# Delta-rule sequences: the layout of a PSUM bank and the time at which outputs leave it

## The chip, the cores and the metric

The kernel runs on one core of a Trainium2 chip. The metric is the device time of one execution in microseconds (us). A core has a matrix engine (TensorE, PE in the profile, its weight loads PEld), a vector engine (DVE), a scalar engine (ACT), GpSimd (POOL) and a queue engine (SP) that issues DMAs. Each engine works through its own instructions in order and waits for others by semaphores. [...]

## The reference

A decoder trunk of four layers over 1024 tokens of width 1024. The token mixers are a gated convolution (layers 0 and 3), a diagonal state-space layer (1) and RWKV-7 time mixing (2). Each layer ends with a gated addition and a LayerNorm. The change is in layer 2, whose core is a recurrence over tokens with a 64x64 state per head, 16 heads:

```python
def _rwkv_step(state, inp):
    r_t, w_t, k_t, v_t, kk_t, a_t = inp
    sa = jnp.einsum("bhvk,bhk->bhv", state, -kk_t)
    state = (state * w_t[:, :, None, :] + sa[..., None] * (kk_t * a_t)[:, :, None, :]
             + v_t[..., None] * k_t[:, :, None, :])
    out = jnp.einsum("bhvk,bhk->bhv", state, r_t)
    return state, out
```

The outputs are then normalised over the 64 values of each head and token (`mu_o`, `var_o`), scaled, joined with a bonus term and gated.

## The kernel before

Layer 2 treats the tokens in two halves of 512 (`h`) and the heads in eight pairs (`m`), so there are 16 sequences. A sequence is eight chunks of 64 tokens (`c`), with the two heads of the pair side by side. The recurrence in a chunk is written as matrices, in four generators per pair:

- `prep` makes the products within a chunk (`scr`, the L1982 matmuls), transposes `kb` to `kbt` (L2006) and prepares `uv` (L2017).
- `tsolve` solves a triangular system on DVE.
- `join` (L2057) assembles that inverse as `tt` with the matmuls `zp` (L2076) and `tp` (L2084). It then opens two PSUM banks `p1`, each with a small matmul by `zero` (L2094). The product of `tt` and `uv` is put into them (L2100), and the matmuls `a2` (L2106) give the part that ACT copies into `ra` (L2109).
- `seq` (L2114) runs the chunks one after the other. For each, `p1` gets `ra` times the state (L2127), ACT copies one half of its rows back as the chunk's `uv` (L2128), `p2` is `kbt` times `uv` (L2131), and two DVE instructions put `p2` into the state `st` (L2134). The next chunk's `p1` needs that state, so this is a chain PE, ACT, PE, DVE.

The parity `w = c % 2` decides which 64 partitions hold a chunk's `uv` and which its output. One bank holds the four even chunks, the other the four odd ones, so both are open from `join` to the end of `seq`. After the last chunk, 16 matmuls with `scr` (L2141) complete the outputs of all eight, and ACT copies them to `o` (L2144).

Behind that come eight squares with sums (`gsq`, L2155), an addition on POOL (`gn_q`, L2156), an inverse root on ACT and DVE, a multiplication of `o` on POOL (L2162), transposes on PE (`otp`, L2169), a scaling on ACT (`yt`), two POOL operations and a DMA out. `o`, `gsq` and `yt` share the tag `t_u` with two buffers.

While the sequence of pair `m-1` runs, the program works on pair `m`: projections (`sp`, 128x512 matmuls of L326 to L328, three for each product), `prep` and `tsolve`. The tile scheduler sets the order on each engine from priorities: `prio(..., PJ)` for `prep` and `join` and `prio(..., PS)` for `seq`, with 600 and 300. After the last pair of the first half come the projections of the second half (`pwa`, L1640), after that of the second half the output projection `op` and the gate `gp`, with POOL adds `rp` (L920).

Of the kernel before, what the change touches and what calls it, by code (L numbers as in the profile page):

```python
# [8 lines left out]
F32 = mybir.dt.float32  # L9
# [6 lines left out]
P = 128  # L16
NB = 8
T = 1024
HT = 512
# [1902 lines left out]
def inner_setup(S, rg, T_):  # L1922
    nc = S.nc
    V, G, SC = nc.vector, nc.gpsimd, nc.scalar
# [21 lines left out]
    rows_b = (slice(0, 64), slice(64, P))  # L1946
    rows_k = (slice(64, P), slice(0, 64))
# [3 lines left out]
    def aux(nm):  # L1951
        return S.paux.tile([P, HT], F32, tag="aux", name=nm)

    def sq(nm):
        return S.pseq.tile([P, HT], F32, tag="sq", name=nm)

    zero = rg.tile([P, 2], F32, tag="zero", name="zero")
# [99 lines left out]
    def join(m, h, R):  # L2057
        ra, ti = R.ra, R.ti
        tt = slot(S, ("a0", "a1")[h], "tt")
        tt = R.tt = tt.rearrange("p (h c) -> p h c", h=8)  # L2060
# [13 lines left out]
        for e in range(8):  # L2074
            for w in range(2):
                nc.tensor.matmul(ps[w][q1[w], e * 32:(e + 1) * 32], R.m10[q0[w], e, :], t1[q0[w], e, :],  # L2076
                                 start=True, stop=True)
# [4 lines left out]
        for e in range(8):  # L2082
            for w in range(2):
                nc.tensor.matmul(ps[w][q0[w], e * 32:(e + 1) * 32], zs[q1[w], e, :], tt[q1[w], e, 32:64],  # L2084
                                 start=True, stop=True)
# [3 lines left out]

        an = R.ant.rearrange("p (c s) -> p c s", c=4)  # L2090
        r5 = ra.rearrange("p (c w) s -> p c w s", w=2)
        R.p1 = [S.pseq.tile([P, 4, P], F32, tag="p1", name="p1", bufs=2) for w in range(2)]
        for w in range(2):
            nc.tensor.matmul(R.p1[w][:, 0, 0:2], S.ident, zero, start=True, stop=False, skip_group_check=True)  # L2094
        ps = [aux("a2"), aux("a2")]
        for c2 in range(4):
            for hd in range(2):
                for w in range(2):
                    rb, cs = rows_b[w], slice(hd * 64, hd * 64 + 64)
                    nc.tensor.matmul(R.p1[w][rb, c2, cs], tt[rb, 2 * c2 + hd, :], R.uv[w][rb, c2, cs],  # L2100
                                     start=False, stop=False, skip_group_check=True)
        for c2 in range(4):
            for hd in range(2):
                for w in range(2):
                    rb = rows_b[w]
# [8 lines left out]
    def seq(m, h, R, dVT, dST, dBV, dZ, dY):  # L2114
# [2 lines left out]
            G.memset(st, 0.0)  # L2117
        else:
            nc.sync.dma_start(st, dST[m][:])
        ot = S.tmp.tile([P, HT], F32, tag="t_u", name="o")  # L2120
        o4 = ot.rearrange("p (c s) -> p c s", c=4)
        for c in range(8):
            w, c2 = c % 2, c // 2
            rb = rows_b[w]
            uv = R.uv[w][:, c2, :]
            p1 = R.p1[w][:, c2, :]
            nc.tensor.matmul(p1, R.ra[:, c, :], st, start=False, stop=False, skip_group_check=True)  # L2127
            SC.copy(uv[rb, :], p1[rb, :])  # L2128
            yield
            p2 = sq("p2")  # L2130
            last = nc.tensor.matmul(p2[:, 0:P], R.kbt[c // 4][:, c % 4, :], uv, start=True, stop=True)  # L2131
            for hd in range(2):
                cs = slice(hd * 64, hd * 64 + 64)
                V.scalar_tensor_tensor(st[cs, cs], st[cs, cs], R.pc[cs, c:c + 1], p2[cs, cs], ALU.mult, ALU.add)  # L2134
            yield
        with S.tc.issue_after(last.ins):
            for c2 in range(4):
                for hd in range(2):
                    for w in range(2):
                        cs = slice(hd * 64, hd * 64 + 64)  # L2140
                        nc.tensor.matmul(R.p1[w][rows_k[w], c2, cs], R.scr[w][:, c2, hd, :], R.uv[w][:, c2, cs],  # L2141
                                         start=False, stop=True, skip_group_check=True)
        for w in range(2):
            SC.copy(o4[rows_k[w]], R.p1[w][rows_k[w]])  # L2144
        if h == 0:
            nc.sync.dma_start(dST[m][:], st)

# [1 line left out]
        o = ot.rearrange("p (g v) -> p g v", v=64)  # L2149
# [56 lines left out]
```

## Time and profile before

| what | value |
|---|---|
| median of three runs | 2838.6 us (2838.0 to 2841.43) |
| the profiled execution | 2839.38 us, span 2837.7 us |
| mean granted TensorE clock | 0.963 |
| first and last p1 of the sequences | 1348.1 and 2106.0 us from the span's start |
| output copies L2144 | 32, of 580 ns |
| squares L2155 | 128, of 241 ns |

A row of waits gives an instruction, whom it waited for, the total in us, the number of waits and the longest. A timeline row gives start, duration, engine, line, operation, what it writes and reads, and in brackets the idle time of its engine ahead of it. Buffer numbers are left out, so `p` stands for p1 at L2127 and for p2 at L2131. A matmul of fp32 data leaves two records.

### The profile page before, as it was taken

The page shows a single profiled execution, that of the slowest core. Times are in us where ns is not written, and L with a number is a line of the kernel's source. Part 1 is how long each engine was busy: PE and PEld are TensorE (multiplying, and loading weights), DVE is VectorE, ACT ScalarE, POOL GpSimd, SP SyncE. Part 2 cuts the span into 40 slices and gives each one's busy share as a digit, 9 for nine tenths or more (in the row PEclk, how much of TensorE's full clock was granted, in tenths as well). Part 3 has the DMA queues.
Part 4 walks back from the last instruction along what each step waited for, and adds up shares of the span by engine and source line. Part 5 has one row for each costly group of instructions (what it writes and reads, how often), then busy time and mean ns, then how long its engine had stood idle before and what let it go on. Part 6 is the DMA issues. An engine that isn't in the chain of part 4 may idle for free.

```text
span 2837.7 us, 40655 instructions
## 1 busy us (share of the span) xinstructions
PE 2681.3 (94%) x14939; PEld 2127.4 (75%) x14939; DVE 1994.8 (70%) x3584; ACT 1163.1 (41%) x2211; POOL 646.9 (23%) x696
## 2 busy tenths in 40 slices
PE   8999999999999999899888799898889999999998
PEld 6877788778877888576667567666768777887887
DVE  6787865477657346888888667888756678876544
ACT  3333322242135223656555476555534343224332
POOL 1143422221116132203333110333232211111000
PEclk9999999999999999999997799999699999999999
DMA  5333322347884333473222245223234433324511
GB/s 168 98 97 97 95 75 66 89 142 212 220 240 140 104 94 122 117 233 107 78 85 87 63 151 170 84 91 89 78 100 135 144 111 111 108 71 129 171 64 38
DMA packets 463128, 331.56 MB, mean 117 GB/s; under 512 B 49449, under 2 KB 398929, under 8 KB 462929
## 3 DMA queue, kind: packets, MB, share of 16 engines
q1 hardware_dynamic: 462928, 328.96, 38.3%
q8 instruction: 118, 1.93, 0.3%
q14 instruction: 82, 0.66, 0.1%
HBM read 250.77 MB, written 77.59 MB: 116 GB/s over the span
## 4 chain that ended last, share of the span: by engine, by line
PE 70%; DVE 16%; ACT 4%; issue 4%; DMA 3%; POOL 3%; SPq 0%; DVEq 0%; POOLq 0%; ACTq 0%
PE op L327 3%; PE op L326 3%; PE op L328 3%; PE gp L328 3%; PE gp L327 3%; PE gp L326 3%; PE sp L326 3%; PE sp L327 3%; PE sp L328 2%; DVE tv L2048 2%; PE qa L508 2%; PE qa L506 2%; PE qa L507 2%; PE zp L326 2%; PE zp L328 2%
## 5 line engine op out<-in xcount | busy, mean ns | idle before, releaser
L299 DVE TENSOR_TENSOR wl<-wraw,wh 128x1024 fp32r<-128x1024 f32 x255 | 331.1, 1299 | 217.9 <-ACT wh L298 214.2
L298 ACT CAST wh<-wraw 128x1024 fp32r<-128x1024 f32 x255 | 267.5, 1049 | 517.7 <-PE gp L327 191.5
L905 POOL TENSOR_TENSOR ln_s<-ln_s,rp 128x512 f32<-128x512 f32 x42 | 60.0, 1429 | 209.8 <-DVE rp L901 209.8
L2134 DVE SCALAR_TENSOR_TENSOR state<-state,pc,p 64x64 f32<-64x64 f32 x256 | 71.1, 278 | 46.9 <-PE p L2131 42.1
L2048 DVE TENSOR_TENSOR tv<-ti,mi 128x128 f32<-128x128 f32 (+3 forms) x128 | 97.8, 764 | 2.4
L2127 PE MATMUL p<-state,ra 128*128 128x128 f32 x256 | 65.6, 343 | 28.8 <-DVE state L2134 26.7
L2128 ACT COPY uv<-p 64x128 f32<-64x128 f32 x128 | 33.1, 259 | 136.5 <-PE p L2127 135.8
L2127 PEld LDWEIGHTS p<-state,ra 128*128 128x128 f32 x256 | 45.8, 217 | 54.1 <-DVE state L2134 44.0
L1982 PEld LDWEIGHTS s<-ra,kb 64*128 64x128 f32 x512 | 64.7, 213 | 20.4 <-ACT scr L1988 6.2
L1982 PE MATMUL s<-ra,kb 64*128 64x128 f32 x512 | 75.2, 314 | 4.1 <-DVE kb L1738 1.9
L328 PE MATMUL gp<-r_0h,wl 128*128 128x512 f32 x192 | 77.5, 404 | 0.0
L327 PE MATMUL gp<-r_0l,wh 128*128 128x512 f32 x192 | 76.8, 400 | 0.0
L326 PE MATMUL gp<-r_0h,wh 128*128 128x512 f32 x192 | 76.6, 399 | 0.0
L326 PE MATMUL gp<-r_1h,wh 128*128 128x512 f32 x192 | 76.4, 398 | 0.0
L920 POOL TENSOR_TENSOR rp<-r_0h,r_0l 128x512 f32<-128x512 f32 x24 | 36.3, 1544 | 174.9 <-PE op L327 174.9
L328 PE MATMUL gp<-r_1h,wl 128*128 128x512 f32 x192 | 76.1, 396 | 0.1
L2131 PE MATMUL p<-uv,kbt 128*128 128x128 f32 x256 | 66.8, 347 | 9.9 <-ACT uv L2128 9.8
L327 PE MATMUL gp<-r_1l,wh 128*128 128x512 f32 x192 | 75.6, 394 | 0.0
L2131 PEld LDWEIGHTS p<-uv,kbt 128*128 128x128 f32 x256 | 44.5, 212 | 37.7 <-ACT uv L2128 31.9
L1991 POOL TENSOR_TENSOR scr<-scr,mask 128x512 f32<-128x512 f32 x32 | 46.0, 1436 | 55.4 <-ACT scr L1988 55.2
L326 PE MATMUL sp<-xs0h,wh 128*128 128x512 f32 x128 | 56.1, 438 | 2.6 <-DVE aq L1720 2.2
L327 PE MATMUL sp<-xs0l,wh 128*128 128x512 f32 x128 | 56.0, 437 | 1.9 <-DVE xs0l L195 1.9
(851 smaller groups left out, 8669.6 us busy)
## 6 DMA issues: line engine op xcount, KB each, us to landing
wraw<-in_conv_w_in_dram SPq DMA_DIRECT2D x84, 512.0 KB
wraw<-in_rwkv_w_rkvz_dram SPq DMA_DIRECT2D x64, 512.0 KB
wraw<-in_ple_gate_dram SPq DMA_DIRECT2D x56, 512.0 KB
wraw<-in_conv_w_out_dram SPq DMA_DIRECT2D x24, 512.0 KB
xt<-xd SPq DMA_DIRECT2D x48, 256.0 KB
wraw<-in_ssm_w_in_dram SPq DMA_DIRECT2D x21, 512.0 KB
xd<-rp SPq DMA_DIRECT2D x40, 256.0 KB
wraw<-in_rwkv_w_out_dram SPq DMA_DIRECT2D x16, 512.0 KB
```

Source lines behind the costliest of these rows:

```text
L298: nc.scalar.copy(wh, raw)
L299: nc.vector.tensor_tensor(wl, raw, f32(wh[:]), ALU.subtract)
L326: nc.tensor.matmul(ps, lh, xh, start=(n == 0), stop=False)
L327: nc.tensor.matmul(ps, lh, xl, start=False, stop=False)
L328: nc.tensor.matmul(ps, ll, xh, start=False, stop=(n == kt - 1))
L506: nc.tensor.matmul(ps, wh[:, k0 + k, :], xh, start=first and k == 0, stop=False, skip_group_check=True)
L905: nc.gpsimd.tensor_tensor(s, s, rs, ALU.add)
L1982: nc.tensor.matmul(pss[hd][:, c * P:(c + 1) * P], kb[rows, 2 * c + w, :], ra[rows, 2 * c + w, :], start=True, stop=True)
L2048: V.tensor_tensor(tv, ti[:, b:8, 4 * b:4 * b + 4].unsqueeze(2).to_broadcast([P, n, c, 4]), mi[:, 4 * b:4 * b + 4, 0:c].rearrange("p q c -> ...
L2127: nc.tensor.matmul(p1, R.ra[:, c, :], st, start=False, stop=False, skip_group_check=True)
L2131: last = nc.tensor.matmul(p2[:, 0:P], R.kbt[c // 4][:, c % 4, :], uv, start=True, stop=True)
L2134: V.scalar_tensor_tensor(st[cs, cs], st[cs, cs], R.pc[cs, c:c + 1], p2[cs, cs], ALU.mult, ALU.add)
```

## The change

A PSUM bank `p1` now holds chunks 0 to 3 of both parities, and a second one chunks 4 to 7. A function `bank` in `seq` opens one and puts the products of `tt` and `uv` into it; the first is opened at the start of `seq`, the second within it, behind chunk 2's copy. `join` no longer touches p1. After chunk 3 and after chunk 7, eight matmuls complete the outputs of four chunks, and ACT copies them to `o` in two pieces of 64x256. `o` gets a tag of its own with two buffers, and the scratch for dynamic DMAs in SBUF is set to 1024 bytes per partition, where the default stood.

```diff
--- before.py
+++ after.py
@@ -2089,16 +2089,7 @@
 
         an = R.ant.rearrange("p (c s) -> p c s", c=4)
         r5 = ra.rearrange("p (c w) s -> p c w s", w=2)
-        R.p1 = [S.pseq.tile([P, 4, P], F32, tag="p1", name="p1", bufs=2) for w in range(2)]
-        for w in range(2):
-            nc.tensor.matmul(R.p1[w][:, 0, 0:2], S.ident, zero, start=True, stop=False, skip_group_check=True)
         ps = [aux("a2"), aux("a2")]
-        for c2 in range(4):
-            for hd in range(2):
-                for w in range(2):
-                    rb, cs = rows_b[w], slice(hd * 64, hd * 64 + 64)
-                    nc.tensor.matmul(R.p1[w][rb, c2, cs], tt[rb, 2 * c2 + hd, :], R.uv[w][rb, c2, cs],
-                                     start=False, stop=False, skip_group_check=True)
         for c2 in range(4):
             for hd in range(2):
                 for w in range(2):
@@ -2117,31 +2108,47 @@
             G.memset(st, 0.0)
         else:
             nc.sync.dma_start(st, dST[m][:])
-        ot = S.tmp.tile([P, HT], F32, tag="t_u", name="o")
+        ot = rg.tile([P, HT], F32, tag="o", name="o", bufs=2)
         o4 = ot.rearrange("p (c s) -> p c s", c=4)
+
+        def bank(ph):
+
+            p1 = S.pseq.tile([P, 2, 2, P], F32, tag="p1", name="p1", bufs=2)
+            nc.tensor.matmul(p1[:, 0, 0, 0:2], S.ident, zero, start=True, stop=False, skip_group_check=True)
+            for c2 in range(2):
+                for hd in range(2):
+                    for w in range(2):
+                        rb, cs = rows_b[w], slice(hd * 64, hd * 64 + 64)
+                        nc.tensor.matmul(p1[rb, w, c2, cs], R.tt[rb, 2 * (2 * ph + c2) + hd, :],
+                                         R.uv[w][rb, 2 * ph + c2, cs], start=False, stop=False, skip_group_check=True)
+            return p1
+        p1s = [bank(0)]
         for c in range(8):
-            w, c2 = c % 2, c // 2
+            w, c2, ph = c % 2, c // 2, c // 4
             rb = rows_b[w]
             uv = R.uv[w][:, c2, :]
-            p1 = R.p1[w][:, c2, :]
+            p1 = p1s[ph][:, w, c2 % 2, :]
             nc.tensor.matmul(p1, R.ra[:, c, :], st, start=False, stop=False, skip_group_check=True)
             SC.copy(uv[rb, :], p1[rb, :])
             yield
+            if c == 2:
+                p1s.append(bank(1))
             p2 = sq("p2")
             last = nc.tensor.matmul(p2[:, 0:P], R.kbt[c // 4][:, c % 4, :], uv, start=True, stop=True)
             for hd in range(2):
                 cs = slice(hd * 64, hd * 64 + 64)
                 V.scalar_tensor_tensor(st[cs, cs], st[cs, cs], R.pc[cs, c:c + 1], p2[cs, cs], ALU.mult, ALU.add)
+            if c % 4 == 3:
+                with S.tc.issue_after(last.ins):
+                    for k in range(2):
+                        for hd in range(2):
+                            for w in range(2):
+                                cs = slice(hd * 64, hd * 64 + 64)
+                                nc.tensor.matmul(p1s[ph][rows_k[w], w, k, cs], R.scr[w][:, 2 * ph + k, hd, :],
+                                                 R.uv[w][:, 2 * ph + k, cs], start=False, stop=True, skip_group_check=True)
+                for w in range(2):
+                    SC.copy(o4[rows_k[w], 2 * ph:2 * ph + 2, :], p1s[ph][rows_k[w], w])
             yield
-        with S.tc.issue_after(last.ins):
-            for c2 in range(4):
-                for hd in range(2):
-                    for w in range(2):
-                        cs = slice(hd * 64, hd * 64 + 64)
-                        nc.tensor.matmul(R.p1[w][rows_k[w], c2, cs], R.scr[w][:, c2, hd, :], R.uv[w][:, c2, cs],
-                                         start=False, stop=True, skip_group_check=True)
-        for w in range(2):
-            SC.copy(o4[rows_k[w]], R.p1[w][rows_k[w]])
         if h == 0:
             nc.sync.dma_start(dST[m][:], st)
 
@@ -2192,7 +2199,7 @@
     import concourse.bacc as _bacc
     from concourse.bass_utils import run_bass_kernel_spmd as _run
 
-    nc = _bacc.Bacc("TRN2", target_bir_lowering=False, num_devices=1)
+    nc = _bacc.Bacc("TRN2", target_bir_lowering=False, num_devices=1, dynamic_dma_scratch_size=1024)
     arrays, aps = {}, {}
     for name in _INS:
         a = _np.ascontiguousarray(inputs[name])
```

The scheduler orders the engines anew, from the first sequence to the end of layer 2. Three places show how. The numbers behind `p_` tell buffers apart.

PE in pair 4 of the second half, from the p1 matmul of chunk 0 to that of chunk 1. Before:

```order
L2127 MATMUL p_18065<-state,ra 128x128
L1716 MATMUL pss<-c_ones,sq 128x2 x4
L2169 MATMUL otp<-ident,o 128x128 x4
L2131 MATMUL p_18165<-uv,kbt 128x128
L1734 MATMUL prn<-ident,rnb 128x128 x4
L1745 MATMUL antp<-ident,aq 128x128
L2127 MATMUL p_18066<-state,ra 128x128
```

In the change (p1 is L2131, p2 is L2137, the bank's first products L2122):

```order
L2131 MATMUL p_18167<-state,ra 128x128
L2122 MATMUL p_18210<-uv,tt 64x64 x2
L1716 MATMUL pss<-c_ones,sq 128x2 x4
L328 MATMUL sp<-xs0h,wl 128x512
L326 MATMUL sp<-xs0h,wh 128x512
L2137 MATMUL p_18179<-uv,kbt 128x128
L327 MATMUL sp<-xs0l,wh 128x512
L328 MATMUL sp<-xs0h,wl 128x512
L326 MATMUL sp<-xs0h,wh 128x512
L1734 MATMUL prn<-ident,rnb 128x128
L2131 MATMUL p_18167<-state,ra 128x128
```

Three projection matmuls now stand between p2 and the next p1, and two ahead of p2; the transposes `otp` of the pair before no longer stand there.

PE at the end of pair 6 of the first half, where `zp`, `tp` and the products into p1 belong to the join and start of pair 7. Before, among the last output matmuls (L2141):

```order
L2141 MATMUL p_14282<-uv,scr 64x64
L2141 MATMUL p_14281<-uv,scr 64x64
L2141 MATMUL p_14282<-uv,scr 64x64
L2076 MATMUL zp<-t_14550,m_14094 32x32 x16
L2141 MATMUL p_14281<-uv,scr 64x64
L2141 MATMUL p_14282<-uv,scr 64x64
L2084 MATMUL tp<-tt,t_14550 32x32 x16
L2094 MATMUL p_14594<-zero,ident 128x2
L2094 MATMUL p_14595<-zero,ident 128x2
L2100 MATMUL p_14594<-uv,tt 64x64 x3
L2100 MATMUL p_14595<-uv,tt 64x64 x3
L2100 MATMUL p_14594<-uv,tt 64x64
```

In the change, from p2 of chunk 5 (output matmuls are L2147, `a2` is L2097):

```order
L2137 MATMUL p_14438<-uv,kbt 128x128
L2131 MATMUL p_14375<-state,ra 128x128
L2137 MATMUL p_14475<-uv,kbt 128x128
L2076 MATMUL zp<-t_14564,m_14106 32x32 x16
L2131 MATMUL p_14375<-state,ra 128x128
L2084 MATMUL tp<-tt,t_14564 32x32 x16
L2137 MATMUL p_14512<-uv,kbt 128x128
L2147 MATMUL p_14375<-uv,scr 64x64 x4
L2097 MATMUL a_14608<-tt,ant 64x64 x3
L2097 MATMUL a_14609<-tt,ant 64x64 x3
```

`zp` and `tp` moved from behind the sequence into its last chunk, and the `a2` matmuls follow half of the output matmuls; before, they stood behind both bank openings and 16 products into p1.

ACT at the end of pair 1 of the first half, from the copy `ra` ahead of the outputs. Before:

```order
L1741 COPY ra<-aq 128x4x2x64
L298 CAST wh<-wraw 128x1024
L1988 COPY scr<-s_12281 128x4x64
L1988 COPY scr<-s_12280 128x4x64
L2144 COPY o<-p_11924 64x512
L2144 COPY o<-p_11925 64x512
L2008 COPY kbt<-kbtp 128x512 x2
L2155 ACTIVATE gsq,gn_q<-o 128x64 x4
L2021 COPY uv<-wps 64x512 x2
L2079 COPY t_12337<-zp 32x256
L2155 ACTIVATE gsq,gn_q<-o 128x64
L2079 COPY t_12337<-zp 32x256
```

In the change (the output copy is L2150, the squares L2162):

```order
L1741 COPY ra<-aq 128x4x2x64
L1988 COPY scr<-s_12285 128x4x64
L1988 COPY scr<-s_12284 128x4x64
L2150 COPY o<-p_12047 64x256 x2
L2162 ACTIVATE gsq,gn_q<-o 128x64 x2
L2008 COPY kbt<-kbtp 128x512 x2
L2162 ACTIVATE gsq,gn_q<-o 128x64 x2
L1590 ACTIVATE rs_t<-gn_q 128x8
L1591 ACTIVATE gn_s<-rs_t 128x8
L2021 COPY uv<-wps 64x512 x2
L2043 COPY ti<-eye 128x256
L2079 COPY t_12341<-zp 32x256 x2
```

Four of the eight squares and two output copies of half the size now stand earlier, at chunk 4 (not shown); of the squares left here all are done ahead of the `uv` copies of `prep`, and the first steps of the root (L1590, L1591) follow at once.

## The prediction

> **What bounds the kernel now.** I read the page first, then windows, waits and the timeline of the stretch that the change touches.
>
> ```profile
> span 2837.7 us, 40655 instructions
> PE 2681.3 (94%) x14939; PEld 2127.4 (75%) x14939; DVE 1994.8 (70%) x3584; ACT 1163.1 (41%) x2211; POOL 646.9 (23%) x696
> PE 70%; DVE 16%; ACT 4%; issue 4%; DMA 3%; POOL 3%; SPq 0%; DVEq 0%; POOLq 0%; ACTq 0%
> q1 hardware_dynamic: 462928, 328.96, 38.3%
> ```
>
> TensorE bounds the whole program: 94% busy, 70% of the chain that ended last. An edit that leaves TensorE's work as it is can win only where TensorE stands idle or runs at a low clock. The delta-rule sequences run from 1348 to 2108 us; these windows show the thin parts (columns: window, length, busy time of PE, PEld, DVE, ACT, POOL, granted clock, DMA):
>
> ```profile
> core 0: us, PE busy (x) PEld busy (x) DVE busy (x) ACT busy (x) POOL busy (x), PEclk, DMA share, GB/s
> 1510.00:1635.00 125.00, 99.94 (x842) 78.21 (x841) 89.04 (x205) 62.00 (x175) 30.47 (x34) 0.69 0.25 75
> 1820.00:1970.00 150.00, 135.77 (x1374) 101.30 (x1368) 129.76 (x296) 87.55 (x244) 52.27 (x53) 1.00 0.28 85
> 1970.00:2054.00 84.00, 72.66 (x618) 59.75 (x617) 64.45 (x155) 43.52 (x124) 25.21 (x23) 0.65 0.29 89
> ```
>
> At full clock a head pair takes 37.5 us (150 for four), with PE 91% and DVE 87% busy; late in each half PE falls to 80-86% at clocks of 0.69 and 0.65. What PE waits for, from 1140 to 2160 us (total, times, longest):
>
> ```profile
> PE p L2127 <- DVE state L2134: 26.7, 29, 2.8
> PE otp L2169 <- POOL o L2162: 13.7, 9, 6.8
> PE p L2131 <- ACT uv L2128: 9.8, 24, 1.0
> PE p L2127 <- ACT ra L2109: 2.0, 6, 0.6
> PE p L2094 <- ACT o L2144: 0.9, 2, 0.7
> ```
>
> The chunk chain itself costs 26.7 + 9.8 us, the output transposes 13.7. The waits that the bank layout causes directly (L2094 for the output copies, p1 for `ra`) are only 2.9 us.
>
> **The change, part by part.** *Work.* TensorE, DVE, POOL and SP keep their instructions, one for one; ACT gains 32, as 32 copies of 64x512 become 64 of 64x256:
>
> ```profile
> L2144 ACT COPY o<-p x32: 578/580/583, 1377.3 to 2109.7; 64x512 f32<-64x512 f32 x32
> L1988 ACT COPY scr<-s x64: 344/372/381, 1300.7 to 2030.9; 128x256 f32<-128x256 f32 x64
> L2155 ACT ACTIVATE gsq<-o x128: 238/241/270, 1379.6 to 2112.1; 128x64 f32<-128x64 f32 x128
> ```
>
> A PSUM copy of 256 columns takes 0.37 us, so ACT pays 64 x 0.37 - 32 x 0.58 = 5.1 us in a stage in which it is 50 to 58% busy. The part on the path is the first half's pair, ahead of chunk 4's or 5's `uv` copy. It runs beside the DVE update between chunks 3 and 4; where nothing else fills that gap (some five sequences) I charge 0.2 us, **+1**; with no cover at all it is 16 x 0.74 = 12 us. The smaller scratch and the own buffer for `o` cost nothing: every data packet above is on the hardware queue, and no wait in the list is one for the old buffer `t_u`.
>
> *Chunk waits.* One step of the chain at full clock:
>
> ```profile
> 1921.84 0.41 PE L2127 MATMUL p<-state,ra 128*128 128x128 f32 x2
> 1922.29 0.26 ACT L2128 COPY uv<-p 64x128 f32<-64x128 f32 x1 [0.26 <-PE p L2127]
> 1922.60 0.49 PE L2131 MATMUL p<-uv,kbt 128*128 128x128 f32 x2
> 1922.85 0.48 PE L326 MATMUL sp<-xs0h,wh 128*128 128x512 f32 x1
> 1923.13 0.59 DVE L2134 SCALAR_TENSOR_TENSOR state<-state,pc,p 64x64 f32<-64x64 f32 x2 [0.16 <-PE p L2131]
> 1923.16 0.39 PE L327 MATMUL sp<-xs0l,wh 128*128 128x512 f32 x1
> 1923.39 0.40 PE L328 MATMUL sp<-xs0h,wl 128*128 128x512 f32 x1
> 1923.86 0.41 PE L2127 MATMUL p<-state,ra 128*128 128x128 f32 x2
> ```
>
> A p1 or p2 holds PE about 0.24 us, a 128x512 matmul 0.23 (the spacing of the rows). From p1's issue end (1922.08) to p2 is 0.5 us; from p2's (1922.85) to the next p1 about 1.0. The stall is whatever of that the other matmuls between them leave open. I took the new order of PE, priced each matmul by its spacing in this trace, and added the shortfall over all 128 p1-p2 gaps and all 112 p2-p1 gaps. With 0.5 us needed: 13.7 us before, 10.0 in the change. With 1.1 us: 26.8 before (measured 26.7), 22.4 in the change. Scaling the measured waits by these ratios gives 9.8 to 7.2 and 26.7 to 22.3: **-7**. The gain comes from head pairs whose p2 stood right behind p1 with no matmul between (pair 4 of the second half: work between first p1 and last p2 grows from 13.4 to 17.6 us). Bounds: 0, if DVE's queue is the pace; -11, if a step needs 1.5 us.
>
> *From one sequence to the next.* The worst case is pair 6 to pair 7 of the first half:
>
> ```profile
> 1625.28 0.80 PE L2131 MATMUL p<-uv,kbt 128*128 128x128 f32 x2 [0.35 <-ACT uv L2128]
> 1626.01 1.76 PE L2141 MATMUL p<-uv,scr 128*64 128x64 f32 x28
> 1627.70 1.06 PE L2076 MATMUL zp<-t,m 32*32 32x32 f32 x32
> 1629.26 1.44 PE L2084 MATMUL tp<-tt,t 32*32 32x32 f32 x32
> 1629.62 1.18 ACT L2144 COPY o<-p 64x512 f32<-64x512 f32 x2
> 1630.63 1.01 PE L2094 MATMUL p<-zero,ident 128*128 128x2 f32 x4
> 1631.57 1.92 PE L2100 MATMUL p<-uv,tt 64*64 64x64 f32 x28
> 1634.97 0.62 PE L2127 MATMUL p<-state,ra 128*128 128x128 f32 x2 [0.30 <-ACT ra L2109]
> ```
>
> From the last p2 to the next first p1 is 9.7 us: the outputs, zp, tp, then the new banks, which wait for both output copies, then 16 matmuls into p1 ahead of the `a2` group that `ra` needs. In the change zp and tp stand inside the last chunk (tp delays that p2 by 1.5 to 2 us), the first bank has long been free, and the `a2` group comes before p1's eight matmuls, which cover the `ra` copy. What is left behind the last p2 is 16 half outputs and `a2` passes and that copy, 4 to 5 us: net **-3** (0 to -5). Of pairs 3 to 4 and 4 to 5, where the priced work behind the last p2 shrinks by 1.6 and 3.2 us with PE partly idle, I take **-2** (-5 to +1).
>
> *The output transposes.* A normal case:
>
> ```profile
> 1924.62 0.49 PE L2131 MATMUL p<-uv,kbt 128*128 128x128 f32 x2
> 1932.29 0.45 POOL L2156 TENSOR_SCALAR gn_q<-gn_q 128x8 f32<-128x8 f32 x1 [4.58 <-ACT gsq L2155]
> 1934.61 1.04 POOL L2162 TENSOR_TENSOR o<-o,gn_s 128x512 f32<-128x512 f32 x1 [1.86 <-DVE gn_s L1595]
> 1935.70 0.66 PE L2169 MATMUL otp<-ident,o 128*128 128x128 f32 x4 [0.18 <-POOL o L2162]
> ```
>
> From the last p2 to `otp` is 11.1 us. In the change the first four squares are done before, so the chain loses 4 x 0.24, a shorter copy pair (0.42) and eight matmuls (0.5): 1.9 us. But PE's order moves `otp` forward by 2 to 2.5 us too (priced work behind the last p2: 9.4 to 6.9 here, 9.9 to 8.0 in the first half), and ACT has a weight cast of 1 us between the two small steps of the root. So I expect a little more stall, **+2** (-3 to +18). The longest one stays:
>
> ```profile
> 2107.06 10.18 POOL L920 TENSOR_TENSOR rp<-r_0h,r_0l 128x512 f32<-128x512 f32 x7 [11.97 <-PE op L327]
> 2117.19 0.24 POOL L2156 TENSOR_SCALAR gn_q<-gn_q 128x8 f32<-128x8 f32 x1
> 2122.20 1.11 PE L2169 MATMUL otp<-ident,o 128*128 128x128 f32 x4 [6.75 <-POOL o L2162]
> ```
>
> Seven POOL adds (10.18 us) stood ahead of `gn_q`; in the change `gn_q` stands behind the first, but the multiplication of `o` still behind all seven.
>
> *Two parities in one bank.*
>
> ```profile
> 1931.10 1.09 PE L2100 MATMUL p<-uv,tt 64*64 64x64 f32 x29
> ```
>
> Its 16 matmuls (two records each, some 0.03 us apart) run fast because neighbours use different halves of the array. In the new order 71 neighbours use the same half, before 38: 33 x 0.055 = **+2** as an estimate from that spacing. [...]
>
> Sum: 1 - 7 - 3 - 2 + 2 + 2 = -7 to -8 us; I take -8. The profiled execution took 2839.4 (span 2837.7 and 1.7 around it), 0.8 above the median of 2838.6, so 2831.4 in its terms and **2830.5** against the median.
>
> **The rivals.** *The idle time only moves* (15%). DVE is 87% busy beside PE's 91%; if state updates queue behind the triangular solve, PE's idle time goes from p1 to the next wait. For it: p1's longest wait, 2.8 us, is far more than the step needs. Against: DVE's work is unchanged, and the late stretches leave it 23 to 29% free. Only the -2 and small change remain: 2837.
>
> *Slower: the transposes come too early* (17%). If the chain behind the last p2 isn't shorter because POOL and ACT serve other work first, as with the 4.58 us that POOL waited for the squares while ACT made the next pair's copies, the 2 to 2.5 us by which `otp` moved forward become stall in 11 sequences. It decides once the extra stall is over 0.9 us a sequence (the 8 of gain and the 2 charged, over 11). At 1.7 us each: 11 x 1.7 = 19 in place of the 2, so 2830.5 + 17 = 2847.5.
>
> *Much faster: the clock* (18%). Pairs 4 and 5 of the second half took 84 us at clock 0.65, where two pairs at full clock take 75. If the 4.2 us of matmuls that move into pair 4 keep the clock up there, and the like happens to one pair of the first half, 9 to 14 us more go: 2819. [...]
>
> **How the numbers follow.** Forecast 50%, own range 2822 to 2838. What can be told from no change is 0.2%, 5.7 us: faster means under 2832.9, slower over 2844.3. Two thirds of the forecast lie under 2832.9 (0.35), with the clock 0.18 and a bit of the first rival: faster 0.55, same 0.26, slower 0.19. The range takes in the clock case to 2814 and most of the slower one: 2814 to 2847.
>
> **What would show it.** Waits of p1 for the state near 22 us and of p2 for `uv` near 7; pair 6 to 7 near 7 us; `otp` near 16, with the last still near 7; 16 groups of p1's first matmuls at most 0.3 us longer. The forecast is wrong if `otp` grows beyond 22 us, if p1's wait stays at 26, or if clocks in the late windows leave 0.6 to 0.75.

## The result and the profile after

The changed kernel takes 2819.2 us in the median (2817.0 to 2820.9, 4 runs); the kernel before, timed on the same chip beside it, 2840.0 (2838.0 to 2843.4). The ratio is 0.9925, 95% interval 0.9908 to 0.9942. The forecast of 2830.5 had the sign right and the size not: 8 us were expected, 20.8 were gained. The time is that of the rival "much faster: the clock" (2819), though only part of it came in that rival's way.

The page of the changed kernel, its span and the busy time of its engines:

```profile
span 2817.1 us, 40692 instructions
PE 2673.0 (95%) x14939; PEld 2119.2 (75%) x14939; DVE 2009.8 (71%) x3584; ACT 1168.8 (41%) x2243; POOL 644.9 (23%) x696
```

The granted clock of TensorE over the whole span, of the kernel before and then of the change:

```profile
core 0: 2837.7 us, clock 0.963
```

```profile
core 0: 2817.1 us, clock 0.966
```

These rows split the gain. PE was not busy for 2837.7 - 2681.3 = 156.4 us before and for 144.1 us after: 12.3 us less. The clock is either full or half (every record of it is 1.0 or 0.5), so a mean of 0.963 is a half clock for 2 x 0.037 x 2837.7 = 210 us, and 0.966 one for 192 us. 128x512 matmuls in a row (L326 to L328) start 231 ns apart at full clock and 427 at half, in both profiles, so a stretch at half clock costs at most about half its length, which is the estimate used here: about 9 us less. Together that is 21 us, and the spans differ by 20.6. What is left, span less idle less half of the half-clock time, is 2576 and 2577 us: PE's own work did not change.

This is the split of one profiled execution of each kernel, and rows that give the clock to 0.001 leave 2.8 us of half-clock time open either way. The spans and clocks of all runs differ more: in the mean 221 us at half clock in 33 runs of the kernel before, 189 in the four of the change, and 180 in twelve with those of e3 and e5 below, which run the same order. Counted at a half, that is 16 to 20 of the 20.8 us. But from run to run of one and the same kernel (97 runs) the span grew by only 0.27 us for each further us at half clock, and counted at that it is 9 to 11. So the clock made between 9 and 20 us of the gain, and shorter waiting made the rest.

What PE waits for from 1140 to 2160 us, in the change (total, times, longest):

```profile
PE p L2131 <- DVE state L2140: 31.0, 27, 3.0
PE kbtp L2006 <- POOL kb L2001: 13.2, 10, 2.0
PE p L2137 <- ACT uv L2132: 8.6, 18, 1.6
PE otp L2176 <- POOL u L528: 8.0, 1, 8.0
PE otp L2176 <- POOL o L2169: 7.2, 9, 1.4
```

The chunk chain did not get shorter: p1 waits 31.0 us for the state, before 26.7. Among what is gone are waits that the forecast never looked at. Three rows of the same view of the kernel before, which have shrunk to 0.2 us or have no row any more in the change:

```profile
PE pb L1759 <- POOL kpl L1757: 6.0, 5, 1.5
PE kbtp L2006 <- ACT scr L1988: 4.0, 6, 0.9
PE sp L326 <- DVE aq L1720: 2.2, 1, 2.2
```

They belong to the preparation and the projections of the next pair, not to the sequence: 12 us in which PE waited for POOL, ACT and DVE. They don't stand in one place: 4.5 us of those for `kpl` lie inside the sequences of the second half, where p1's wait grew, and three of those for `scr`, 1.8 us, directly behind sequences of the first half. Three windows of the change show where the time fell (window, length, busy time of PE, PEld, DVE, ACT, POOL, granted clock, DMA):

```profile
1338.80:1647.80 309.00, 275.97 (x2482) 206.83 (x2483) 250.42 (x569) 177.97 (x496) 88.24 (x97) 0.85 0.27 84
1801.50:2062.50 261.00, 227.02 (x2244) 175.42 (x2240) 224.13 (x505) 144.15 (x410) 81.57 (x81) 0.92 0.30 92
1952.50:2062.50 110.00, 95.55 (x880) 74.46 (x878) 90.53 (x207) 56.02 (x159) 28.23 (x27) 0.83 0.35 106
```

The same stretches of the kernel before, which hold nearly the same PE work:

```profile
1340.00:1665.00 325.00, 277.47 (x2481) 211.80 (x2482) 246.39 (x568) 173.22 (x475) 88.75 (x96) 0.83 0.26 80
1820.00:2086.00 266.00, 238.17 (x2269) 183.52 (x2263) 219.31 (x505) 144.70 (x403) 82.05 (x81) 0.89 0.30 91
1970.00:2086.00 116.00, 102.40 (x896) 82.22 (x895) 89.55 (x211) 57.15 (x160) 29.78 (x28) 0.75 0.32 99
```

The first half's sequences lost 16 us, nearly all of it idle time (47.5 to 33.0 in these windows). The second half lost 5, there PE's busy time fell by 11, at a better clock and with 25 matmul records fewer in the window, and its idle time rose by 6.

### The profile page after: what moved, and what is told of

Same layout as the page of the kernel before. It is cut to its first block, busy times and chain, and to the rows that moved or that the text cites. A ratio compares the mean times of both kernels' runs of the same rounds, so it can differ in the third digit from the quotient of the medians.

```text
span 2817.1 us, 40692 instructions
## 1 busy us (share of the span) xinstructions
PE 2673.0 (95%) x14939; PEld 2119.2 (75%) x14939; DVE 2009.8 (71%) x3584; ACT 1168.8 (41%) x2243; POOL 644.9 (23%) x696
## 4 chain that ended last, share of the span: by engine, by line
PE 71%; DVE 15%; issue 4%; ACT 4%; DMA 3%; POOL 3%; SPq 0%; DVEq 0%; POOLq 0%; ACTq 0%
PE op L327 3%; PE op L326 3%; PE op L328 3%; PE gp L328 3%; PE gp L327 3%; PE gp L326 3%; PE sp L326 2%; PE sp L327 2%; PE sp L328 2%; PE qa L506 2%; PE qa L507 2%; PE qa L508 2%; DVE tv L2048 2%; PE zp L326 2%; PE zp L328 2%
## 5 line engine op out<-in xcount | busy, mean ns | idle before, releaser
L2048 DVE TENSOR_TENSOR tv<-ti,mi 128x128 f32<-128x128 f32 (+3 forms) x128 | 97.1, 759 | 2.5
L2131 PE MATMUL p<-state,ra 128*128 128x128 f32 x256 | 65.2, 341 | 31.3 <-DVE state L2140 31.0
L2131 PEld LDWEIGHTS p<-state,ra 128*128 128x128 f32 x256 | 45.2, 213 | 54.8 <-DVE state L2140 49.2
L328 PE MATMUL gp<-r_0h,wl 128*128 128x512 f32 x192 | 77.2, 402 | 0.0
L326 PE MATMUL gp<-r_0h,wh 128*128 128x512 f32 x192 | 76.6, 399 | 0.0
L326 PE MATMUL gp<-r_1h,wh 128*128 128x512 f32 x192 | 76.4, 398 | 0.0
L328 PE MATMUL gp<-r_1h,wl 128*128 128x512 f32 x192 | 76.0, 396 | 0.2 <-DVE wl L299 0.2
L2137 PE MATMUL p<-uv,kbt 128*128 128x128 f32 x256 | 66.2, 344 | 8.7 <-ACT uv L2132 8.6
L2137 PEld LDWEIGHTS p<-uv,kbt 128*128 128x128 f32 x256 | 44.9, 210 | 36.6 <-ACT uv L2132 31.3
```

The lines of the kernel that those rows point to most:

```text
L326: nc.tensor.matmul(ps, lh, xh, start=(n == 0), stop=False)
L328: nc.tensor.matmul(ps, ll, xh, start=False, stop=(n == kt - 1))
L2048: V.tensor_tensor(tv, ti[:, b:8, 4 * b:4 * b + 4].unsqueeze(2).to_broadcast([P, n, c, 4]), mi[:, 4 * b:4 * b + 4, 0:c].rearrange("p q c -> ...
```

## The experiments

The theories at the start, as the expectations name them. **A**: the new order of the join (the `a2` matmuls ahead of the bank's opening and its products) is what pays. **B**: the outputs that leave the tail pay, by the squares (B1), by the copies of `o` with the bank that they release (B2), or by the eight output products (B3). Most edits also make the scheduler place other rows anew, on PE from some 280 records (e4) to over 4000 of 14939 (the change itself, e7, and e10 against e11), so a verdict is always on an edit together with that.

**e1: the kernel before, with the join's order of the change.**

```diff
-        R.p1 = [...]            # two banks opened, 16 products into them
-        ...
         ps = [aux("a2"), aux("a2")]
         ...                     # a2 matmuls and the copies of ra
+        R.p1 = [...]            # the same behind the copies of ra
```

> The kernel before with one thing changed: in join the a2 matmuls and the copies into ra come first, and opening both banks and the 16 products into p1 come behind them. Banks by parity, outputs all at the end. Theory A (the order in join, which takes the p1 products and the wait for the banks off the way to the next sequence, carries the gain): 2825 to 2830 us, and the gaps from a sequence's last p2 to the next first p1 shrink by 3 us or more in the first half. Theory B (outputs, squares and banks that are done after chunk 3 carry it): 2836 to 2840, gaps as before. Theory C (any new order of the scheduler would have moved the time by this much): no telling, plus or minus 10.

2842.1 us beside 2837.1: ratio 1.0013 (1.0000 to 1.0027). A is false.

**e2: the change, with all outputs behind chunk 7.**

```diff
-            if c % 4 == 3:
-                ...             # eight products, two copies of this half
             yield
+        for ph in range(2):
+            ...                 # the same for both halves
```

> The changed kernel with the outputs of all eight chunks behind chunk 7: 16 output matmuls and four copies there, both banks busy to the end; the bank layout, the banks opened in the sequence and the a2 matmuls ahead of p1 stay. Theory B: most of the gain is lost, 2833 to 2838 us, and the transposes come some 2 us later behind the last p2. Theory A: 2820 to 2825.

2852.2 us, ratio 1.0051 (1.0036 to 1.0067). With this part undone the change is slower than the kernel before, so the new bank layout alone does not pay: the gain hangs on the outputs that leave the tail. PE's idle time is lower than in the kernel before all the same, 147.7 us; what e2 loses it loses at half clock, 251 us.

**e3: the change, with `o` back in the shared buffer and the larger DMA scratch.**

```diff
-        ot = rg.tile([P, HT], F32, tag="o", name="o", bufs=2)
+        ot = S.tmp.tile([P, HT], F32, tag="t_u", name="o")
...
-    nc = _bacc.Bacc("TRN2", ..., num_devices=1, dynamic_dma_scratch_size=1024)
+    nc = _bacc.Bacc("TRN2", ..., num_devices=1)
```

> The changed kernel with o in the old tag t_u (two buffers for o, gsq and yt) and the default scratch; the order on every engine is word for word that of the changed kernel, so only waits for a buffer can differ. Theories A, B and C: within 2 us of the changed kernel, 2817 to 2822. If o's own buffer is what helps (a first half of o would have to wait for the last pair's yt to leave): 2826 or more.

2816.6 us, ratio 0.9930 (0.9915 to 0.9945), the change's own. Buffer and scratch cost and bring nothing.

**e4: the kernel before, with the priority of the sequence at 305 in place of 300.** An edit with no meaning of its own, to see how far a new order alone moves the time.

```diff
-PS, PT, PJ = 300, 300, 600
+PS, PT, PJ = 305, 300, 600
```

> The kernel before with the priority of the sequences at 305 in place of 300: the same work and data flow, another order (463 lines of difference on PE). A control for theory C. Theories A and B: 2836 to 2844. Theory C: off by 8 us or more in either direction.

2839.4 us, ratio 1.0013 (1.0001 to 1.0025): no sign that any new order helps. It is a weak control: it moves some 280 records of PE and 50 of ACT, the change some 4400 and 1080.

**e5: the change, with the squares meant to be late.**

```diff
-        for g in range(8):
-            SC.activation(gsq[:, g, :], ...)
+        with S.tc.issue_after(last.ins):
+            for g in range(8):
+                SC.activation(gsq[:, g, :], ...)
```

> The changed kernel with all eight squares issued only behind the last p2; output matmuls and copies of the first half stay early, and so does the freed bank. Theory B1 (the squares that ACT no longer has to do at the end are what helps: 4 x 0.24 us less in its queue there, and gn_q ahead of the next pair's POOL work): half of the 20 us or more goes, 2828 to 2838. Theory B2 (the bank and the copies that are done early help): 2817 to 2823.

2813.3 us, ratio 0.9916 (0.9901 to 0.9931). I first read this as "B1 is not needed". It shows nothing of the kind: `last` is a matmul, the hold orders only instructions of PE, and the squares are ACT's. The instructions stand in the order of the change on all five engines, but for some matmuls that start within 0.3 us of each other; the first four squares of pair 0 still run 9 us ahead of the last p2. So e3 and e5 are two more measurements of the change: 0.9925, 0.9930, 0.9916. Their half-clock times were 192, 186 and 169 us: 6 us of span between equal orders is what this kernel's clock does by itself.

**e6: the change, with the copies meant to be late.**

```diff
-                for w in range(2):
-                    SC.copy(o4[rows_k[w], 2 * ph:2 * ph + 2, :], p1s[ph][rows_k[w], w])
             yield
+        with S.tc.issue_after(last.ins):
+            for ph in range(2):
+                for w in range(2):
+                    SC.copy(o4[rows_k[w], 2 * ph:2 * ph + 2, :], p1s[ph][rows_k[w], w])
```

> The changed kernel with the first half's output matmuls still behind chunk 3, but all four output copies, and so the squares, behind the last p2; the first bank stays busy to the end. Theory B1: like the run with late squares, within 3 us. Theory B2: 6 us or more slower than that run. Theory B3 (the eight output matmuls that leave the end help): near the changed kernel, 2817 to 2823, though squares and copies are late.

2806.3 us, ratio 0.9890 (0.9874 to 0.9907). The hold failed in the same way: the first copies of `o` still run 12 us ahead of the last p2 of pair 0. What did change is the order around the last two pairs of the program, and one wait, that of the last transposes:

```profile
PE otp L2178 <- POOL u L528: 1.0, 1, 1.0
```

8.0 us in the change, 1.0 here. On POOL `gn_q` (at 2082.46 us) and the multiplication of `o` (2084.94) now stand ahead of the additions `rp` (from 2087.23). The last stall, which the forecast had left as it was, can be had; e8 and e12 come back to it.

**e7: the change, with the first bank opened in the join, ahead of the `a2` matmuls.**

```diff
     def join(m, h, R):
         ...
+        R.p1s = [bank(R, 0)]
         ps = [aux("a2"), aux("a2")]
     def seq(...):
-        p1s = [bank(0)]
+        p1s = R.p1s
```

> The changed kernel with the first bank opened, and its eight products made, in join ahead of the a2 matmuls, as the old kernel had it. If the order in join adds to the early outputs: 3 to 8 us slower than the changed kernel, 2822 to 2828; if it is worth nothing, as the run with a2 first alone says: 2817 to 2821.

2805.1 us, ratio 0.9883 (0.9868 to 0.9899). The change's order of the join is not only no gain, the old one with the new layout is a little better.

**e8: the change, with the multiplication of `o` of the last pair of each half on DVE.**

```diff
-        G.tensor_tensor(o, o, bcs(s1), ALU.mult)
+        (V if m == NB - 1 else G).tensor_tensor(o, o, bcs(s1), ALU.mult)
```

> The changed kernel with the multiplication of o for the last pair (both halves) on DVE in place of POOL, so that it no longer stands behind the adds of rp: the longest wait of PE, 8.0 us ahead of the last transposes, goes to 1 us or less, and the time to 2810 to 2814. If PE then waits as long for what follows: 2817 to 2820.

2809.1 us, ratio 0.9904 (0.9889 to 0.9918). Some of that came at a better clock (0.972); the last stall stayed. Its row:

```profile
PE otp L2176 <- DVE o L2169: 8.0, 2, 7.5
```

So POOL's queue alone was not what held the multiplication. What did is seen in DVE's timeline of the change at that place, in the steps of the root between `gn_q` and `o`:

```profile
2091.58 1.21 DVE L946 TENSOR_SCALAR gn_q<-gn_q 128x8 f32<-128x8 f32 x1
...
2098.08 1.19 DVE L952 TENSOR_TENSOR rs_t<-rs_t,gn_q 128x8 f32<-128x8 f32 x1
2099.30 0.17 DVE L953 SCALAR_TENSOR_TENSOR gn_s<-rs_t,gn_s 128x8 f32<-128x8 f32 x1
2099.49 0.17 DVE L951 TENSOR_TENSOR rs_t<-gn_s 128x8 f32<-128x8 f32 x1
```

and in POOL's of the same microseconds:

```profile
2090.22 9.01 POOL L920 TENSOR_TENSOR rp<-r_0h,r_0l 128x512 f32<-128x512 f32 x6
2100.14 1.04 POOL L2169 TENSOR_TENSOR o<-o,gn_s 128x512 f32<-128x512 f32 x1 [0.91 <-DVE gn_s L953]
```

While POOL runs its additions `rp`, from 2090.22 to 2099.23, six of seven DVE steps on 128x8 elements take 1.13 to 1.25 us; the moment they end, the same steps take 0.17. And when POOL is free, it still waits 0.91 us for DVE. The stall is the root's chain, stretched by POOL's work beside it.

With e1 to e8 a new theory seemed to fit. **D**: in every fast kernel the old pair's squares and `gn_q` stand ahead of the next pair's join on ACT and POOL, in every slow one they are mixed with it. **C**: what counts is the length of ACT's tail. **M**: the eight products on PE by themselves (B3). The next three runs were made to tell these apart, the hold now on ACT's own copy of `uv`.

**e9: the kernel before, with only the squares and `gn_q` ahead of the join.**

```diff
+        with S.tc.high_priority(offset=400):
             for g in range(8):
                 SC.activation(gsq[:, g, :], ...)
             G.tensor_scalar(s2, s2, GN_EPS, None, ALU.add)
```

> The kernel before, with nothing of the change: only the eight squares and gn_q of a pair are given precedence over the next pair's join, so that ACT does all eight squares ahead of the join's copies (zp, tp) and POOL does gn_q ahead of the clearing of tt. Theory D (what pays is that the old pair's tail is no longer mixed with the new pair's join): gn_q falls from 8.6 to 13.5 us after the last p2 to about 5, PE's idle time in the first half's sequences from 47 to about 33 us, the ratio to 0.992 to 0.996. Theory C (what pays is that half of ACT's copies and squares leave the tail): nothing leaves it here, so the ratio stays within 0.002 of 1.

2859.4 us beside 2835.8: ratio 1.0080 (1.0064 to 1.0096); PE's idle time in the first half is 41 us, not 33. `gn_q` did come early (6.0 us behind the last p2 in the first pairs, before 9.9 to 10.2), and the kernel got slower. D is false: what the squares gain there the join loses, and the first p1 of the next pair comes 15.5 to 16.9 us behind the last p2 in the first three pairs, before 14.5 to 15.2.

**e10: the change, with only the eight products early.**

```diff
-            SC.copy(uv[rb, :], p1[rb, :])
+            lcp = SC.copy(uv[rb, :], p1[rb, :])
...
+        with S.tc.issue_after(lcp.ins):
+            ...                 # all four copies of o, then all eight squares
```

> The change with the eight output products still at chunk 3, but all four copies of o and all eight squares held on ACT behind the copy of uv of the last chunk (this hold is on ACT itself; in e5 and e6 the hold named an instruction of PE and moved nothing on ACT). ACT and POOL then stand mixed with the next join as in the kernel before. Theories C and D: the gain goes, ratio 0.999 to 1.005 as in e2, PE's idle time in the first half above 42 us. Rival M (the eight products out of the tail pay by themselves): the ratio stays at 0.990 to 0.994 and the idle time at 33.

2872.0 us, ratio 1.0113 (1.0085 to 1.0142): the slowest of all. M did not come about. Nor did the numbers of C and D: the ratio lies above their range, and PE's idle time in the first half is 38 us, not above 42. Its clock row, and ACT's timeline behind the first pair of the first half (the last p2 is at 1374.9):

```profile
core 0: 2871.7 us, clock 0.951
```

```profile
1384.17 0.37 ACT L2079 COPY t<-zp 32x256 f32<-32x256 f32 x1
1384.56 0.21 ACT L1590 ACTIVATE rs_t<-gn_q 128x8 f32<-128x8 f32 x1
1384.68 1.03 ACT L298 CAST wh<-wraw 128x1024 fp32r<-128x1024 f32 x1
1388.39 0.37 ACT L2100 COPY ra<-a 128x256 f32<-128x256 f32 x1 [2.68 <-PE a L2097]
1388.79 0.36 ACT L2087 COPY tt<-tp 32x256 f32<-32x256 f32 x1
1389.18 0.21 ACT L1591 ACTIVATE gn_s<-rs_t 128x8 f32<-128x8 f32 x1
1392.10 0.37 ACT L2100 COPY ra<-a 128x256 f32<-128x256 f32 x1 [2.71 <-PE a L2097]
```

The order on ACT has come out badly: the second copy `tt` stands behind the first copy `ra`, which waits 2.68 us for PE, and starts 0.03 us after its end. The two parities of the join, which run side by side in the change, run one after the other, and the next first p1 comes 18.3 us behind the last p2, in the change 11.7. The same place of the change:

```profile
1381.27 0.75 ACT L2087 COPY tt<-tp 32x256 f32<-32x256 f32 x2 [0.92 <-PE tp L2084]
1382.04 0.78 ACT L2179 ACTIVATE yt<-otp,vec 128x512 f32<-128x512 f32 x1
1382.80 0.65 ACT L2100 COPY ra<-a 128x256 f32<-128x256 f32 x2
```

This happens behind three pairs (18.3, 18.3 and 18.5 us against 11.7, 11.8 and 13.9). PE fills much of these 18 us with other work: over the whole span it idles only 8 us longer than in the change. The clock rows give most of the 55 us between the two spans: 2 x 0.049 x 2871.7 = 281 us at half clock, 90 more than in the change, up to 45 us.

**e11: the change, with only the squares late.**

```diff
+        with S.tc.issue_after(lcp.ins):
             for g in range(8):
                 SC.activation(gsq[:, g, :], ...)
```

> The change with only the squares held on ACT behind the copy of uv of the last chunk; o is still copied in two halves, and on POOL gn_q still stands ahead of the clearing of tt. Theory D: most of the gain stays, ratio 0.991 to 0.995. Theory C (the length of ACT's tail): four squares of about 0.15 us each come back into each of 16 tails, some 10 us, ratio 0.995 to 0.998.

2812.4 us, ratio 0.9918 (0.9901 to 0.9934): the change's own. The four squares that the forecast counted as early work are worth nothing (B1 and C's sum are out; a square follows the one before it after 0.24 us in the rows, so C's four in 16 tails would have been 15 us, not 10). As written, e10 and e11 differ in one thing, the place of the two copies of the first half of `o`: early, 0.9918; late, 1.0113. So of B1 to B3 only B2 is left. The eight kernels here whose first copies of `o` run 7 us or more ahead of the last p2 (the change, e3, e5 to e8, e11, e12) are all faster than the kernel before, and the five others (e1, e2, e4, e9, e10) are not. That is an argument by exclusion: e10 is 32 us slower than the kernel before, which has late copies too, so the bad order of its join is in the comparison beside the copies, and most of what separates it from e11 is the clock. With the early copies goes the bank that they release: behind the first three pairs the next bank opens 7 to 8 us before the last p2 in e11, 1.0 us behind it in e10, and 3.0 us behind it in the kernel before, so the opening alone does not sort the kernels. (PE writes `p` in PSUM, and ACT and DVE read it there, as in `uv<-p` and `state<-state,pc,p`; PE opens a bank again behind ACT's copy of `o` out of it, for which it waits 0.9 us at L2094 in the kernel before, two times, and 0.8 us at L2117 in the change, once.) Whether the copies count because ACT has them out of the way or because PE has the bank early, these runs can't separate; a kernel with a third p1 buffer and late copies would have, and wasn't tried. Nor were the halves in the old banks of one parity, where ACT would read a bank that PE is writing.

**e12: e7, with the last multiplication of `o` ahead of the next layer's `rp` on POOL.**

```diff
-        G.tensor_tensor(o, o, bcs(s1), ALU.mult)
+        om = G.tensor_tensor(o, o, bcs(s1), ALU.mult)
+        if m == NB - 1 and h == 1:
+            S.omul = om.ins
...                             # gate_half
+            with S.tc.issue_after(S.omul):
                 nc.gpsimd.tensor_tensor(rs, f32(rh[:]), f32(rl[:]), ALU.add)
```

> e7 (first bank opened in the join) and, on POOL, the multiplication of o of the very last pair ahead of the next layer's products rp instead of behind seven of them. If the last stall is POOL's queue (the multiplication behind seven products of about 1 us), PE's idle time in the 40 us after the last p2 falls from 8.2 to 1 or 2 us and the time to about 2798, ratio 0.986. If it is the chain itself (copies, squares, root, multiplication), the stall stays near 8 and the time near 2805, ratio 0.988.

2797.0 us beside 2835.8: ratio 0.9856 (0.9842 to 0.9871), the fastest, and 8 us under e7 as forecast. The wait for the last transposes is out of the list (5.6 us over 9, longest 1.3). DVE's steps of the root in e12:

```profile
2075.83 0.17 DVE L949 TENSOR_SCALAR gn_s<-gn_q 128x8 int32<-128x8 int32 x1 [0.16 <-POOL gn_q L2169]
2076.03 0.17 DVE L950 TENSOR_SCALAR gn_q<-gn_q 128x8 f32<-128x8 f32 x1
```

0.17 us each, since the additions now run behind the multiplication. My expectation put the stall down to POOL's queue; e8 had taken that away without effect, so it is POOL's work beside DVE's that e12 removed.

## Why the prediction was right or wrong

**What bounds the kernel** held: PE's own work is 2576 us before and 2577 after, and all of the gain is idle time and clock. The terms of the sum make -7; -8 was taken.

**The chunk waits, -7** (p1 26.7 to 22.3, p2 9.8 to 7.2): wrong in the larger part. p1's wait is 31.0, p2's 8.6, so +3 instead of -7. By halves p1's wait fell from 21.2 to 13.3 us in the first and rose from 5.5 to 17.8 in the second. The step that failed is the pricing of the gaps from the order of PE alone, with DVE's answer held fixed: it gave one ratio for the whole program, and the two halves went opposite ways. DVE's answer did change. In the second half 26 of the 56 state updates between chunks start more than 0.5 us behind the end of their p2, before 15; 17.1 of p1's 17.8 us of waiting there follow such an update, and in 20 of the 33 us by which these updates are late DVE works at the triangular solve (L2048, L2053, L2054). One of them in pair 3 of the second half:

```profile
1936.19 0.49 PE L2137 MATMUL p<-uv,kbt 128*128 128x128 f32 x2
1936.52 0.72 DVE L2054 TENSOR_TENSOR ti<-ti,td 128x56 f32<-128x56 f32 x1
1937.27 0.75 DVE L1720 SCALAR_TENSOR_TENSOR aq<-sp,c_om,pt 128x512 f32<-128x512 f32 x1
1937.93 0.70 DVE L2048 TENSOR_TENSOR tv<-ti,mi 128x128 f32<-128x128 f32 x1
1938.67 0.28 DVE L2053 TENSOR_REDUCE td<-tv 128x32 f32<-128x128 f32 x1
1938.99 0.19 DVE L2054 TENSOR_TENSOR ti<-ti,td 128x32 f32<-128x32 f32 x1
1939.10 0.58 DVE L2140 SCALAR_TENSOR_TENSOR state<-state,pc,p 64x64 f32<-64x64 f32 x2
1939.73 0.49 PE L2131 MATMUL p<-state,ra 128*128 128x128 f32 x2 [2.12 <-DVE state L2140]
```

The forecast named this case as a bound, "0, if DVE's queue is the pace". A longer wait of p1 is not its full price, though: while it grew by 12.3 us in the second half, PE's idle time there grew by 5.4, since other waits went.

p1's wait at 31.0 is one of the three signs that the forecast named as its own undoing, "if p1's wait stays at 26". A second, the clock of the late windows, came about for one of them: pairs 4 and 5 of the second half, 0.65 before, run at 0.78; the late window of the first half is at 0.72 (1492.52 to 1612.77 us).

**From one sequence to the next, -3 and -2**: the named place was right. From the last p2 of pair 6 to the next first p1 it was 9.3 us and is 3.7 (a gain of 5.6; about 7 us were forecast for the gap), from pair 4 to 5 it went from 5.8 to -1.5, the next first p1 ahead of the last p2. But that was read at four pairs. Behind pairs 0, 1 and 5 the gap fell from 15.2, 14.5 and 21.6 us to 11.7, 11.8 and 13.8 too. PE's idle time in the seven gaps of the first half fell from 9.5 to 1.7 us, and in those of the second half it rose from 1.7 to 5.6: -3.9 together, near the -5 that was forecast, but made of other gaps. No step of the sum looked at what the tail of one pair does to the preparation of the next, and e10 and e11 tie that to the early copies of `o`.

**The sum.** PE's idle time from the first p1 to the last p2 of a half went from 47.1 to 32.5 us in the first half and from 28.9 to 34.3 in the second, -9.2 together. That this is near the forecast's -8 is partly luck, since its largest term had the wrong sign. What made the gain larger than forecast is a term that the sum put at nothing: the clock, 9 to 20 us.

**Output transposes, +2**: 13.7 to 15.2 us, +1.5, and the last one "still near 7" is 8.0. The size held. The reason given for the last one, POOL's queue, was half of it (e8, e12).

**Two parities in one bank, +2**: the products into p1 in the groups of the profile's page, before and then in the change (busy time, mean ns of one, idle time before them):

```profile
L2100 PE MATMUL p<-uv,tt 64*64 64x64 f32 x512 | 27.5, 259 | 0.0
```

```profile
L2122 PE MATMUL p<-uv,tt 64*64 64x64 f32 x512 | 28.8, 252 | 0.0
```

+1.3 us for 512 records. Neighbours on the two row halves, now writing one bank, still start 2 to 7 ns apart (133 of the 512 records start within 7 ns of the one before, in the kernel before 134).

**ACT's extra copies, +1, and the buffer and the scratch, 0**: e3 shows the second; the copies are not only hidden, without half of them early there is no gain (e2, e10).

**The rivals.** "Idle only moves" named the mechanism that the second half shows, state updates behind the triangular solve, and the chunk waits did move from the first half to the second; it is false of the total, which fell by 12.3 in the profiled executions. "Transposes too early" did not happen. "The clock" gave the time of 2819, and some of its mechanism: pairs 4 and 5 of the second half take 78.4 us, 83.7 before, and the half-clock time of all sequences went from 161 to 133 us; that the matmuls moved into pair 4 kept the clock up there is not shown. By the clock the gain is 9 to 20 us, forecast in that rival were 9 to 14, and the idle time is the rest, so the agreement with 2819 is partly chance. The forecast's own term for the clock was nothing, though it separates the kernels of this study as much as waiting does.

## What to carry to other kernels

Where one engine is 94% busy and its clock is halved now and then, as here, compare two versions by busy time, idle time and half-clock time of the whole span before you look for a cause; a sum of waits alone misses the clock's part. Between pipelined stages look at what the tail of one holds back in the next, above all a buffer that is released late and in-order engines whose queue mixes both. And look at the order that an edit really gives: two holds here named an instruction of the wrong engine, held nothing on ACT, and read like a result.

## What was not expected of the hardware

**The clock also fell behind windows in which PE had work.** In the profiles of the kernel before and of the change, the 23 and 21 half-clock stretches are 1 to 13 times 3.41 us long, but for the last of each, which the end of the program cuts. In the change, the window ahead of such a start at 1508.26, the one behind it, and the rest of that stretch:

```profile
1504.85:1508.26 3.41, 0.80 (x4) 0.42 (x4) 3.15 (x6) 2.44 (x7) 3.41 (x4) 1.00 0.86 264
1508.26:1511.67 3.41, 2.69 (x16) 2.29 (x17) 3.33 (x5) 1.07 (x2) 3.41 (x3) 0.50 0.96 314
1511.67:1552.63 40.96, 37.69 (x283) 30.90 (x282) 29.78 (x74) 20.97 (x62) 9.72 (x12) 0.50 0.22 72
```

and one in the kernel before, ahead of a start at 1973.19:

```profile
1969.78:1973.19 3.41, 2.19 (x16) 1.61 (x14) 3.25 (x13) 1.82 (x5) 1.04 (x1) 1.00 0.00 0
```

PE was busy for 0.80 and for 2.19 of 3.41 us when the clock fell. Between 1140 and 2160 us of these two profiles, the 3.41 us ahead of a fall had PE 56% busy in the median of the 18 falls before and 47% in that of the 15 in the change, so a few short waits in one window can go with a fall; single windows lie anywhere from 0 to 96%, so the busy time of that window alone does not decide it. In the change the clock then stayed down for 44 us, with PE 92% busy in the last 41 of them. The return has a clearer sign: the last window of every half-clock stretch there had PE 89% busy or more. But 33 of the 70 other windows at half clock were as full, and the clock did not return behind them. What brings the fall and the return is not shown here.

**Small DVE steps beside POOL's additions take seven times as long**: 1.2 us against 0.17 for 128x8 elements, shown in the rows under e8 and e12. Such a step takes about as long as one of the additions, of which this one stands alone in the timeline of the change:

```profile
2088.76 1.30 POOL L920 TENSOR_TENSOR rp<-r_0h,r_0l 128x512 f32<-128x512 f32 x1 [16.43 <-PE op L327]
```

L946, with one input, took 1.21 us beside them, and L952, with two, 1.19. What couples the two engines is not shown here.

**The slow and the fast kernels here differ by the clock as much as by waiting.** From the spans, busy times and clocks of six profiled executions, one of each kernel, worked out as in the section on the result:

| kernel | span | PE not busy | at half clock | span - idle - half of that |
|---|---|---|---|---|
| before | 2837.7 | 156.4 | 210 | 2576 |
| change | 2817.1 | 144.1 | 192 | 2577 |
| e9, squares first | 2854.2 | 145.0 | 263 | 2578 |
| e10, only products early | 2871.7 | 152.0 | 281 | 2579 |
| e11, squares late | 2818.2 | 134.6 | 197 | 2585 |
| e12, bank in join, `o` first | 2795.0 | 127.6 | 168 | 2584 |

From 128 to 156 us idle, from 168 to 281 us at half clock, and a rest that stays within 9 us. e9 and e10 wait no more than the kernel before and lose their time to the clock. The runs of all kernels say the same more strongly: the mean span less half of the mean half-clock time is 2723 to 2727 us for the kernel before, the change, e1 to e5 and e8 to e10, whose spans lie from 2808 to 2869; only e6, e7, e11 and e12 are lower, 2719, 2716, 2719 and 2710. With the clock counted at a half, the upper end of its price, the first group differs by the clock alone. What sets how long a half clock lasts stays open.
